# Weight tiles at fourteen addresses modulo 512 in a decoder layer on TensorE

## The chip, the cores and the metric

One NeuronCore of a Trainium2 chip runs the whole layer. The metric is the device time of one execution in microseconds (us). The engines are named as the profile names them: PE (TensorE matmuls), PEld (TensorE weight loads), DVE (VectorE), ACT (ScalarE), POOL (GpSimd) and SP, whose queue issues most DMAs.

## The reference

One layer of a hybrid decoder on x of 256 tokens by 2048 channels, all in float32:

```python
x = layer_norm(alpha * x + 0.5 * swiglu(x, w_gate1, w_up1, w_down1))        # d_ff = 5632
p = x @ w_in                                                                # 2048 x 6432
o_attn = diff_attn_group(p[..., :3072])      # 8 heads: softmax(s1) - lam * softmax(s2), then RMS norm
o_rwkv = rwkv7_group(p[..., 3072:])          # 16 heads of 64, delta-rule state over 256 tokens
x = layer_norm(alpha * x + concat(o_attn, o_rwkv) @ w_out)
x = layer_norm(alpha * x + 0.5 * swiglu(x, w_gate2, w_up2, w_down2))
```

Nearly all arithmetic is in the eight large products with weights; there are 350 MB of weights, read once.

## The kernel before, in words

**Split products.** Each float32 operand of a large product is split into a high and a low part of the type fp32r. A product is three matmuls: high x high (L105), low weight x high activation (L106), high weight x low activation (L107). The activations are the stationary operand (128 x 128, loaded by a weight load of PE), the weights the moving one (128 x 512). The two halves of 128 tokens are called tt 0 and tt 1.

**The weight stream.** `Stream.block` walks down a column of 512 weight columns in steps of two 128-row pieces. In each step SP loads a tile `raw` (512 KB), ACT rounds it to `wh` (L128), DVE subtracts to get `wl` (L129), and `mm` issues six matmuls for tt 0. The six for tt 1 come up to four steps later (`LAG`), so that PE reads two steps' buffers in turn. `raw` has 3 buffers, `wh` and `wl` 7 each (`NW`). A step thus takes 12 large matmuls, and there are 5856 with activations `xh` and `xl` as stationary operand (gate, up, `w_in`, `w_out`) and 2112 with the hidden activations `hh` (down).

**Stages.** FFN 1: gate and up blocks in turn, each pair ending in four transposes of `h` per token half (L221) and a split into `hh` tiles; then four down blocks; this twice, for 6 and for 5 groups of 512 hidden channels. Then the mixer: `w_in` blocks, with attention (`attn_heads`) and RWKV (`rwkv_group`) work put between the steps of the stream, and `w_out`. Then FFN 2 as FFN 1.

**Attention.** Two generators take two heads each and run in turn. A head's output goes from PSUM through `ot`: ACT squares into it (L803), DVE clips into it (L804), ACT squares it (L806), DVE writes the normed output (L817), PE transposes it (L821), DVE puts it over the query tile (L822). A scheduler orders each engine's instructions.

**Addresses.** Tiles lie at a byte address within each partition, and pools hand out addresses one tag after the other, so a tag's size sets the address of all that follow. One 128 x 128 slice of a stationary tile is 512 bytes, one piece of a weight tile 2048 bytes, so all slices of a tile have one address modulo 512:

| tiles | before | after |
|---|---|---|
| `xh`, `xl` (all 16) | 64 | 64 |
| `hh` J0, J1, J2 (both token halves), H0, H3 | 32 | 64 |
| `hh` H1, H4, H2, H5 | 64 | 64 |
| `raw` (3) | 64 | 64 |
| `wh` (7) | 64 | 64, 128, 192, ... 448 |
| `wl` (7) | 64 | 96, 160, 224, ... 480 |
| `ident` (moving tile of the transposes) | 128 | 128 |
| `h` (stationary tile of L221) | 480 | 416 |

Before, H3 has 4112 bytes in the mixer (`praw`), and that moves what follows from 32 to 64. In a block of a down stage, four of six (or four of five) groups of hidden channels are in tiles at 32. Of the 2112 matmuls of these stages 1536 have their stationary tile at 32 and 576 at 64.

Of the kernel before, what the change touches and what calls it, by code (L numbers as in the profile page):

```python
# [10 lines left out]
F32 = mybir.dt.float32  # L11
F32R = mybir.dt.float32r
# [4 lines left out]
P = 128  # L17
D = 2048
S = 256
DFF = 5632  # L20
NB = 512
# [10 lines left out]
NW = 7  # L32
# [5 lines left out]
def build(tc, A, out):  # L38
# [3 lines left out]
    hp = ctx.enter_context(tc.tile_pool(name="hp", bufs=1))  # L42
    xp = ctx.enter_context(tc.tile_pool(name="xp", bufs=1))
    wp = ctx.enter_context(tc.tile_pool(name="wp", bufs=1))
    sp = ctx.enter_context(tc.tile_pool(name="sp", bufs=2))
    dp = ctx.enter_context(tc.tile_pool(name="dp", bufs=1, space=bass.MemoryType.DRAM))
    pa = ctx.enter_context(tc.tile_pool(name="pa", bufs=3, space=bass.MemoryType.PSUM))

    HT = {"lw": "H0", "T1": "H1", "T2": "H2", "k": "H4"}
    uid = [0]  # L50

    def nm(s):
        uid[0] += 1
        return f"{s}_{uid[0]}"
# [31 lines left out]
    class Stream:  # L86
# [24 lines left out]
        def block(self, src, c0, w, ks, lhs, done, budget=0.0):  # L111
            blk = dict(ks=ks, w=w, lhs=lhs, done=done)
            for ki in range(0, len(ks), 2):
                for f in self.hooks.get(self.step, ()):
                    f()
                self.step += 1
                n = 2
                r0 = ks[ki][0]
                raw = wp.tile([P, n, NB], F32, tag="raw", name=nm("raw"), bufs=NRAW)
                wh = wp.tile([P, n, NB], F32R, tag="wh", name=nm("wh"), bufs=NW)  # L120
                wl = wp.tile([P, n, NB], F32R, tag="wl", name=nm("wl"), bufs=NW)
                g = 1 if self.step == 1 else n
                for k in range(0, n, g):
                    c = slice(k, k + g)
                    nc.sync.dma_start(out=raw[:, c, :w], in_=src[(r0 + k) * P:(r0 + k + g) * P, c0:c0 + w].rearrange("(k p) n -> p k n", p=P))
                for k in range(0, n, g):
                    c = slice(k, k + g)
                    SC.copy(out=wh[:, c, :w], in_=raw[:, c, :w])  # L128
                    V.tensor_tensor(out=wl[:, c, :w], in0=raw[:, c, :w], in1=wh[:, c, :w].bitcast(F32), op=ALU.subtract)  # L129
                st = (blk, ki, n, wh, wl)  # L130
                self.mm(st, 0)
                self.pend.append(st)
                if len(self.pend) > max(0, min(LAG, self.step // 4 - 1)):
                    self.mm(self.pend.pop(0), 1)
                self.run_bg(budget)
# [38 lines left out]
    def ln_tail(tt, y, st, gt, bt, last):  # L174
        mv = sp.tile([P, 2], F32, tag="mv", name=nm("mv"))
        V.bn_aggr(out=mv, in_=st)
        ve = sp.tile([P, 1], F32, tag="ve", name=nm("ve"))
        V.tensor_scalar(out=ve, in0=mv[:, 1:2], scalar1=LN_EPS, scalar2=None, op0=ALU.add)
        rs = sp.tile([P, 1], F32, tag="rs", name=nm("rs"))
        G.tensor_tensor(out=rs, in0=ve, in1=neghalf, op=ALU.pow)  # L180
        for q in range(4):
            c = slice(q * NB, (q + 1) * NB)
            yq = y[q]
            V.scalar_tensor_tensor(out=yq, in0=yq, scalar=mv[:, 0:1], in1=gt[:, c], op0=ALU.subtract, op1=ALU.mult)  # L184
            V.scalar_tensor_tensor(out=yq, in0=yq, scalar=rs, in1=bt[:, c], op0=ALU.mult, op1=ALU.add)  # L185
            if last:
                nc.sync.dma_start(out=out[tt * P:(tt + 1) * P, c], in_=yq)
            else:
                transpose_split(yq, tt, q, xT)
                nc.scalar.dma_start(out=xs[tt][:, c], in_=yq)  # L190

    def load_gb(pool, g, b, tg, tb, after=None):
        gt = (hp if tg == "J0" else pool).tile([P, D], F32, tag=tg, name=nm("lng"))
        bt = pool.tile([P, D], F32, tag=tb, name=nm("lnb"))
        if after is not None:
            G.tensor_copy(out=gt[:, 0:1], in_=after)
            G.tensor_copy(out=bt[:, 0:1], in_=after)
        nc.gpsimd.dma_start(out=gt, in_=g.to_broadcast([P, D]))
        nc.gpsimd.dma_start(out=bt, in_=b.to_broadcast([P, D]))
        return gt, bt  # L200

    def ffn(fp, wg, wu, wd, lg, lb, res, last, extra=None):
        y = [fp.tile([P, D], F32, tag=f"y{t}", name=nm("y")) for t in range(2)]
        st = [sp.tile([P, 4, 6], F32, tag=f"st{t}", name=nm("st"), bufs=1) for t in range(2)]
        gb = []
        j0 = 0
        for half, nj in enumerate((6, 5)):
            hT = {}
            sg = {}

            def gate_done(tt, acc):
                s = fp.tile([P, NB], F32, tag="sg", name=nm("sg"), bufs=2)
                SC.activation(out=s, in_=acc, func=AF.Silu)  # L213
                sg[tt] = s

            def up_done(tt, acc, j):
                h = fp.tile([P, NB], F32, tag="h", name=nm("h"), bufs=2)
                V.scalar_tensor_tensor(out=h, in0=sg[tt], scalar=0.5, in1=acc, op0=ALU.mult, op1=ALU.mult)  # L218
                tr = tr_bank[-1]()
                for i in range(4):  # L220
                    T.transpose(tr[:, i, :], h[:, i * P:(i + 1) * P], ident)  # L221
                if j < 3:
                    if tt == 0:
                        hT[j] = hp.tile([P, 4, 4, P], F32R, tag=f"J{j}", name=nm("hh"))
                    hi, lo = hT[j][:, 2 * tt], hT[j][:, 2 * tt + 1]
                else:
                    hl = hp.tile([P, 2, 4, P], F32R, tag=f"H{3 * tt + j - 3}", name=nm("hh"))
                    hi, lo = hl[:, 0], hl[:, 1]
                SC.copy(out=hi, in_=tr)  # L229
                V.tensor_tensor(out=lo, in0=tr, in1=hi.bitcast(F32), op=ALU.subtract)  # L230
                hT[(tt, j)] = (hi, lo)

            for j in range(nj):
                c0 = (j0 + j) * NB
                stream.block(wg, c0, NB, KX, x_lhs, gate_done)
                stream.block(wu, c0, NB, KX, x_lhs, lambda tt, acc, j=j: up_done(tt, acc, j))

            def h_lhs(tt, k, hT=hT):
                hi, lo = hT[(tt, k // 4)]
                return hi[:, k % 4, :], lo[:, k % 4, :]  # L240

            if half == 0 and extra is not None:
                extra(hT[(0, 0)][0][:, 0, 0:1].bitcast(F32))
            if half == 1:
                gb = load_gb(fp, lg, lb, "lng", "lnb", hT[(0, 0)][0][:, 0, 0:1].bitcast(F32))

            def down_done(tt, acc, n, half=half, hT=hT):
                c = slice(n * NB, (n + 1) * NB)
                if half == 0:
                    rc = fp.tile([P, NB], F32, tag="rc", name=nm("rc"), bufs=2)  # L250
                    G.tensor_copy(out=rc[:, 0:1], in_=hT[(0, 0)][0][:, 0, 0:1].bitcast(F32))
                    nc.scalar.dma_start(out=rc, in_=res[tt][:, c])
                    V.scalar_tensor_tensor(out=y[tt][:, c], in0=rc, scalar=ALPHA, in1=acc, op0=ALU.mult, op1=ALU.add)
                else:
                    V.tensor_tensor(out=y[tt][:, c], in0=y[tt][:, c], in1=acc, op=ALU.add)
                    V.bn_stats(out=st[tt][:, n, :], in_=y[tt][:, c])
                    if n == 3:
                        ln_tail(tt, [y[tt][:, i * NB:(i + 1) * NB] for i in range(4)], st[tt], gb[0], gb[1], last)

            for n in range(4):  # L260
                ks = [(j0 * 4 + k, k) for k in range(nj * 4)]
                stream.block(wd, n * NB, NB, ks, h_lhs, lambda tt, acc, n=n, f=down_done: f(tt, acc, n))
            j0 += nj
# [53 lines left out]
    def mix(mp, pq, C):  # L317
# [434 lines left out]
        def attn_heads(g, st, heads):  # L752
            q, k, vt = st["q"], st["k"], st["v"]
            W = 3 * P
            spans = [slice(0, P), slice(P, W)]
            for h in heads:
# [37 lines left out]
                T.matmul(po[:, 1, :], pT[:, 1, :], vt[0][:, hc], start=True, stop=False)  # L794
                T.matmul(po[:, 1, :], pT[:, 2, :], vt[1][:, hc], start=False, stop=True)

                ot = mp.tile([P, 2, P], F32, tag="ot", name=nm("ot"), bufs=2)
                ss = mp.tile([P, 2, 2], F32, tag="ss", name=nm("ss"), bufs=2)
                vr = mp.tile([P, 2, 2], F32, tag="vr", name=nm("vr"), bufs=2)
                fl = mp.tile([P, 2, 2], F32, tag="fl", name=nm("fl"), bufs=2)  # L800
# [149 lines left out]
```

## Time and profile before

| | |
|---|---|
| time, median of two runs | 2023.2 us (2022.15 and 2024.24) |
| time of the profiled execution | 2021.85 us |
| its span, from the first to the last instruction | 2020.1 us |
| mean granted TensorE clock | 0.989 of full speed |
| PE busy | 1976.9 us, 98% |
| PEld busy | 1614.6 us, 80% |
| DVE, ACT busy | 1149.0 us (57%), 887.6 us (44%) |

A row of a group reads: line, engine, operation, output <- inputs, tile shapes, count, then busy time in us, mean duration of one in ns, and the idle time of the engine just before them with what ended it. Durations of matmuls overlap, since a matmul's end is that of its last result; how fast they go is seen from the starts. A row of the timeline reads: start in us, length in us, engine, line, operation; equal neighbours are merged (x2). Buffer numbers are left out of names.

### The profile page before, as it was taken

Reading aid. Unit: us, or ns where it says so; the run is one execution under the profiler, and the core shown is the slowest. Engines: PE = TensorE matmul, PEld = TensorE weight load, DVE = VectorE, ACT = ScalarE, POOL = GpSimd, SP = SyncE. Lnnn points to the kernel's source line nnn. Section 1 sums busy time; section 2 is a strip of 40 time slices with the busy share of each in tenths; the row PEclk is TensorE's granted clock in tenths of the full one; section 3 lists DMA queues with packets and bytes.
Section 4 is the critical chain, followed back from the end, with each engine's and each line's share of the span. In section 5 each row is a group of like instructions: output and inputs, shape, how many; then the busy total and the mean of one; then the engine's idle time right before and its main releaser. Section 6 shows DMA issues by size and latency. Waiting matters only on the chain. (4 is left out here: it accounts for less than half of the span.)

```text
span 2020.1 us, 24928 instructions
## 1 busy us (share of the span) xinstructions
PE 1976.9 (98%) x9671; PEld 1614.6 (80%) x9671; DVE 1149.0 (57%) x1420; ACT 887.6 (44%) x1100; POOL 33.9 (2%) x68
## 2 busy tenths in 40 slices
PE   9999999999999999999999988999999999999997
PEld 7888888888888878888777777788888888888886
DVE  5555544445554566776677866755554444555455
ACT  5444433344444337645574444444443334444432
POOL 0200000000000000000000000000000000000000
PEclk9999999999999999999999979999999999999999
DMA  7766666667666556556435624666666666766553
GB/s 248 214 188 195 186 190 202 205 192 229 193 187 189 188 171 194 177 160 178 139 86 177 198 84 148 210 198 188 196 185 190 203 204 191 230 193 187 189 188 125
DMA packets 202008, 373.35 MB, mean 185 GB/s; under 512 B 22826, under 2 KB 24944, under 8 KB 201120
## 3 DMA queue, kind: packets, MB, share of 16 engines
q1 hardware_dynamic: 182928, 350.53, 58.0%
q10 hardware_dynamic: 17440, 14.29, 2.4%
q0 software_dynamic: 1520, 6.93, 1.0%
q8 instruction: 76, 1.25, 0.3%
q14 instruction: 44, 0.36, 0.1%
HBM read 364.10 MB, written 7.60 MB: 184 GB/s over the span
## 5 line engine op out<-in xcount | busy, mean ns | idle before, releaser
L129 DVE TENSOR_TENSOR wl<-raw,wh 128x1024 fp32r<-128x1024 f32 (+1 forms) x665 | 808.2, 1216 | 662.4 <-ACT wh L128 661.3
L128 ACT CAST wh<-raw 128x1024 fp32r<-128x1024 f32 (+1 forms) x665 | 695.2, 1046 | 851.9 <-PE acc L107 736.8
L107 PE MATMUL acc<-wh,xl 128*128 128x512 f32 (+1 forms) x1952 | 740.7, 391 | 1.6 <-DVE xl L79 1.6
L106 PE MATMUL acc<-wl,xh 128*128 128x512 f32 (+1 forms) x1952 | 736.7, 392 | 1.0 <-DVE wl L129 1.0
L105 PE MATMUL acc<-wh,xh 128*128 128x512 f32 (+1 forms) x1952 | 725.5, 392 | 9.0 <-ACT xh L78 7.6
L105 PEld LDWEIGHTS acc<-wh,xh 128*128 128x128 f32 x1952 | 367.9, 189 | 88.7 <-ACT xh L78 9.3
L106 PEld LDWEIGHTS acc<-wl,xh 128*128 128x128 f32 x1952 | 368.1, 189 | 77.5 <-issue 2.0
L107 PEld LDWEIGHTS acc<-wh,xl 128*128 128x128 f32 x1952 | 367.8, 188 | 76.3 <-DVE xl L79 2.0
L107 PE MATMUL acc<-wh,hh 128*128 128x512 f32 x704 | 258.0, 395 | 0.0
L106 PE MATMUL acc<-wl,hh 128*128 128x512 f32 x704 | 256.7, 394 | 0.0
L105 PE MATMUL acc<-wh,hh 128*128 128x512 f32 x704 | 256.0, 394 | 0.0
L106 PEld LDWEIGHTS acc<-wl,hh 128*128 128x128 f32 x704 | 132.0, 187 | 31.4
L107 PEld LDWEIGHTS acc<-wh,hh 128*128 128x128 f32 x704 | 132.0, 188 | 31.2
L105 PEld LDWEIGHTS acc<-wh,hh 128*128 128x128 f32 x704 | 132.0, 188 | 30.9
L230 DVE TENSOR_TENSOR hh<-tr,hh 128x512 fp32r<-128x512 f32 x44 | 30.4, 691 | 64.4 <-ACT hh L229 64.4
L229 ACT CAST hh<-tr 128x512 fp32r<-128x512 f32 x44 | 25.8, 586 | 91.7 <-PE tr L221 91.6
L218 DVE SCALAR_TENSOR_TENSOR h<-sg,acc 128x512 f32<-128x512 f32 x44 | 30.3, 688 | 35.6 <-PE acc L107 35.6
L213 ACT ACTIVATE sg<-acc 128x512 f32<-128x512 f32 x44 | 26.4, 600 | 43.8 <-PE acc L107 43.7
L577 DVE TENSOR_TENSOR itmp<-U,Y 64x31 f32<-64x31 f32 (+15 forms) x62 | 20.6, 332 | 11.5 <-DMA U<-dU 10.2
L221 PEld LDWEIGHTS tr<-ident,h 128*128 128x128 f32 x176 | 21.8, 139 | 5.7
L221 PE MATMUL tr<-ident,h 128*128 128x128 f32 x176 | 26.3, 272 | 0.0
L579 DVE TENSOR_TENSOR Y<-Y,itmp 64x31 f32<-64x31 f32 (+15 forms) x62 | 20.6, 332 | 1.4
(247 smaller groups left out, 750.2 us busy)
## 6 DMA issues: line engine op xcount, KB each, us to landing
raw<-in_ffn_w_up_dram SPq DMA_DIRECT2D x176, 512.0 KB, 3.9
raw<-in_ffn_w_down_dram SPq DMA_DIRECT2D x176, 512.0 KB, 4.1
raw<-in_ffn_w_gate_dram SPq DMA_DIRECT2D x175, 512.0 KB, 3.9
raw<-in_w_in_dram SPq DMA_DIRECT2D x96, 512.0 KB, 3.9
raw<-in_w_out_dram SPq DMA_DIRECT2D x32, 512.0 KB, 4.6
rc<-xs ACTq DMA_DIRECT2D x16, 256.0 KB, 4.0
lng<-in_ln_g_dram POOLq DMA_DIRECT2D x3, 1024.0 KB, 7.0
lnb<-in_ln_b_dram POOLq DMA_DIRECT2D x3, 1024.0 KB, 9.3
```

The costliest lines, as they stand in the source:

```text
L105: T.matmul(a, hi, wh[:, j, :w], start=(ki + j == 0), stop=False)
L106: T.matmul(a, hi, wl[:, j, :w], start=False, stop=False)
L107: T.matmul(a, lo, wh[:, j, :w], start=False, stop=(ki + j == last))
L128: SC.copy(out=wh[:, c, :w], in_=raw[:, c, :w])
L129: V.tensor_tensor(out=wl[:, c, :w], in0=raw[:, c, :w], in1=wh[:, c, :w].bitcast(F32), op=ALU.subtract)
L213: SC.activation(out=s, in_=acc, func=AF.Silu)
L218: V.scalar_tensor_tensor(out=h, in0=sg[tt], scalar=0.5, in1=acc, op0=ALU.mult, op1=ALU.mult)
L221: T.transpose(tr[:, i, :], h[:, i * P:(i + 1) * P], ident)
L229: SC.copy(out=hi, in_=tr)
L230: V.tensor_tensor(out=lo, in0=tr, in1=hi.bitcast(F32), op=ALU.subtract)
L577: V.tensor_tensor(out=tv, in0=U[:, 0:j, j:j + 1].to_broadcast([64, j, 32 - j]), in1=Y[:, j:j + 1, j:32].to_broadcast([64, j, 32 - j]), op= ...
L579: V.tensor_tensor(out=Y[:, 0:j, j:32], in0=Y[:, 0:j, j:32], in1=tv, op=ALU.add)
```

## The change

Each of the 7 `wh` and 7 `wl` buffers gets a tag of its own and 32 bytes more than it needs, in the order wh, wl, wh, wl, so that each starts 32 bytes (modulo 512) after the one before. The tag H3 is claimed first in its pool, with the 4128 bytes that it can need at most, and the `hh` tile in it starts 32 bytes in; so all `hh` tiles lie at 64. The 448 bytes and more that this takes are made up for by `ot`, which gets one buffer instead of two.

```diff
+    hp.tile([P, 4 * (S + 2)], F32, tag="H3", name="h3")
...
-                wh = wp.tile([P, n, NB], F32R, tag="wh", name=nm("wh"), bufs=NW)
-                wl = wp.tile([P, n, NB], F32R, tag="wl", name=nm("wl"), bufs=NW)
+                wh, wl = (wp.tile([P, n * NB + 8], F32R, tag=f"{t}{self.step % NW}", name=nm(t))[:, :n * NB].rearrange("p (k n) -> p k n", k=n)
+                          for t in ("wh", "wl"))
...
-                    hl = hp.tile([P, 2, 4, P], F32R, tag=f"H{3 * tt + j - 3}", name=nm("hh"))
-                    hi, lo = hl[:, 0], hl[:, 1]
+                    n = 3 * tt + j - 3
+                    o = 8 if n == 3 else 0
+                    hl = hp.tile([P, o + 8 * P], F32R, tag=f"H{n}", name=nm("hh"))
+                    hi, lo = [hl[:, o + c:o + c + NB].rearrange("p (a b) -> p a b", a=4) for c in (0, NB)]
...
-                ot = mp.tile([P, 2, P], F32, tag="ot", name=nm("ot"), bufs=2)
+                ot = mp.tile([P, 2, P], F32, tag="ot", name=nm("ot"))
```

The order of instructions is the same on every engine up to the middle of the mixer, and again from its end. Between, the single `ot` makes the scheduler put the second head of a pair behind the transposes of the first, and other work moves with it. (In the changed kernel lines stand two to four further down: L129 becomes L131, L804 L808, L821 L825.)

DVE, in the first pair of heads of the second attention group, before (`ot_9278` is the first head's, `ot_9292` the second's):

```order
L814 TENSOR_TENSOR ars_9282<-ars_9282,fl_9281 128x4
L129 TENSOR_TENSOR wl_9718<-raw_9716,wh_9717 128x1024
L804 TENSOR_SCALAR ot_9292<-at_9288 128x256
L815 TENSOR_TENSOR ars_9282<-ars_9282 128x2
L809 TENSOR_SCALAR vr_9294<-ss_9293 128x2
L812 TENSOR_SCALAR fl_9295<-ss_9293 128x2
L603 COPY PT_8548<-sm_8551 32x512
L129 TENSOR_TENSOR wl_9737<-raw_9735,wh_9736 128x1024
L817 TENSOR_SCALAR ot_9278<-at_9274,ars_9282 128x128 x2
```

The same place after (`ot_9279` and `ot_9293`):

```order
L818 TENSOR_TENSOR ars_9283<-ars_9283,fl_9282 128x4
L819 TENSOR_TENSOR ars_9283<-ars_9283 128x2
L821 TENSOR_SCALAR ot_9279<-at_9275,ars_9283 128x128 x2
L131 TENSOR_TENSOR wl_9719<-raw_9717,wh_9718 128x1024
L826 TENSOR_SCALAR qq<-at_9343,ng 128x256
L808 TENSOR_SCALAR ot_9293<-at_9289 128x256
L813 TENSOR_SCALAR vr_9295<-ss_9294 128x2
L816 TENSOR_SCALAR fl_9296<-ss_9294 128x2
L131 TENSOR_TENSOR wl_9738<-raw_9736,wh_9737 128x1024
```

The second head's clip (L804, now L808) stood ahead of the first head's last write to `ot`; now it stands behind that and behind the copy of the transposed first head into `qq`.

PE at the same place, before (L602, L613 and L623 are small products and transposes of the second RWKV group, L821 the transposes of `ot`):

```order
L602 MATMUL sm_8551<-YT_8547,Q 32x32 x32
L613 MATMUL sm_8588<-TT_8541,PT_8548 32x32
L623 MATMUL sm_8643<-ident,BKc 128x64 x8
L821 MATMUL at_9342<-ident,ot_9278 128x128 x2
L613 MATMUL sm_8588<-TT_8541,PT_8548 32x32 x31
L623 MATMUL sm_8653<-ident,BKc 128x64 x8
L623 MATMUL sm_8663<-ident,BKc 128x64 x8
L821 MATMUL at_9364<-ident,ot_9292 128x128 x2
```

And after:

```order
L825 MATMUL at_9343<-ident,ot_9279 128x128 x2
L606 MATMUL sm_8552<-YT_8548,Q 32x32 x32
L617 MATMUL sm_8589<-TT_8542,PT_8549 32x32
L627 MATMUL sm_8644<-ident,BKc 128x64 x8
L825 MATMUL at_9365<-ident,ot_9293 128x128 x2
L770 MATMUL at_9373<-k_8087,qq 128x128
L770 MATMUL at_9373<-k_8087,qq 128x256
L617 MATMUL sm_8589<-TT_8542,PT_8549 32x32 x31
```

The first head's transposes moved ahead of the RWKV group's products, and the second head's transposes ahead of 31 of them.

## The prediction

> **What bounds the kernel now.** The page comes first: the span, the engines' busy time, and the six groups of instructions that hold most of it.
>
> ```profile
> span 2020.1 us, 24928 instructions
> PE 1976.9 (98%) x9671; PEld 1614.6 (80%) x9671; DVE 1149.0 (57%) x1420; ACT 887.6 (44%) x1100; POOL 33.9 (2%) x68
> ...
> L107 PE MATMUL acc<-wh,xl 128*128 128x512 f32 (+1 forms) x1952 | 740.7, 391 | 1.6 <-DVE xl L79 1.6
> L106 PE MATMUL acc<-wl,xh 128*128 128x512 f32 (+1 forms) x1952 | 736.7, 392 | 1.0 <-DVE wl L129 1.0
> L105 PE MATMUL acc<-wh,xh 128*128 128x512 f32 (+1 forms) x1952 | 725.5, 392 | 9.0 <-ACT xh L78 7.6
> ...
> L107 PE MATMUL acc<-wh,hh 128*128 128x512 f32 x704 | 258.0, 395 | 0.0
> L106 PE MATMUL acc<-wl,hh 128*128 128x512 f32 x704 | 256.7, 394 | 0.0
> L105 PE MATMUL acc<-wh,hh 128*128 128x512 f32 x704 | 256.0, 394 | 0.0
> ```
>
> PE is idle for 2020.1 - 1976.9 = 43 us and almost never waits for a split weight. So the time is the number of large matmuls, 3 x 1952 + 3 x 704 = 5856 + 2112 = 7968, times the distance from one start to the next. Only that distance matters, and the mean durations above (391 to 395 ns) are not it, because matmuls overlap. The timeline of PE gives it. First a stretch in a gate or up block, from the first to the thirtieth matmul:
>
> ```profile
> 1408.31 0.39 PE L107 MATMUL acc<-wh,xl 128*128 128x512 f32 x1
> ...
> 1414.89 0.39 PE L107 MATMUL acc<-wh,xl 128*128 128x512 f32 x1
> ```
>
> 29 distances in 6.58 us: **227 ns**. Then a stretch in a down block, at a place where both token halves read J tiles, H0 or H3, thirty distances:
>
> ```profile
> 320.96 0.39 PE L105 MATMUL acc<-wh,hh 128*128 128x512 f32 x1
> ...
> 327.96 0.62 PE L107 MATMUL acc<-wh,hh 128*128 128x512 f32 x2
> ```
>
> 7.00 / 30 = **233 ns**. Same clock, same shapes, no wait in either. What differs is the address of the stationary tile modulo 512: in the gate block moving and stationary tile both lie at 64, an offset (moving minus stationary) of 0; in the down stretch they lie at 64 and 32, an offset of 32. The view of the instructions that use the weight tiles and the hidden tiles says the same in medians (minimum / median / maximum of a duration):
>
> ```profile
> L105 PEld LDWEIGHTS acc<-wh,xh x1952: 186/188/333, 6.8 to 1900.8; 128*128 128x128 f32 x196
> L105 PE MATMUL acc<-wh,xh x1952: 290/389/794, 6.8 to 1901.1; 128*128 128x512 f32 x193, 128*128 128x288 f32 x3
> ```
>
> ```profile
> L105 PEld LDWEIGHTS acc<-wh,hh x704: 187/188/192, 271.5 to 2007.2; 128*128 128x128 f32 x176
> L105 PE MATMUL acc<-wh,hh x704: 389/394/398, 271.8 to 2007.4; 128*128 128x512 f32 x176
> ...
> L106 PE MATMUL acc<-wl,hh x704: 387/394/397, 273.1 to 2007.7; 128*128 128x512 f32 x176
> ```
>
> A duration less 162 ns is the distance to the next start: 389 goes with 227, and 394 goes with 232, the down stages as a whole (1536 of their 2112 matmuls have the offset 32, the others 0). The weight load takes 188 ns in both, so it doesn't simply last longer; the stream of the running matmul is what is stretched while the next stationary tile is read.
>
> **Is 227 the good case or a bad one?** Two things bear on it. One is what happens at offset 0 after a disturbance. Behind eight small fp32 matmuls in the mixer the distances do not return to 227 at once:
>
> ```profile
> 875.63 1.89 PE L461 MATMUL sm<-lw,bones 128*128 128x256 f32 x8
> ...
> 877.59 0.39 PE L107 MATMUL acc<-wh,xl 128*128 128x512 f32 x1
> ...
> 879.67 0.39 PE L107 MATMUL acc<-wh,xl 128*128 128x512 f32 x1
> ```
>
> From 877.59 to 879.67 are nine distances, 2.08 / 9 = 231 ns, and only then does 227 come and stay. I read this as a state that settles: with one constant offset of 0 the stream and the load fall into a step that costs 227; out of step the same addresses cost 231. With the constant offset 32 they settle at 233. The other thing is the last large matmul ahead of a small one, whose stationary tile lies elsewhere. Windows around four of them, ahead of the transposes of h (offset 96), of the product with bones (128), of the transposes of s (480) and of the product with pT (288):
>
> ```profile
> L106 PE MATMUL acc<-wl,xh 128*128 128x512 f32 x1 | 0.4, 389 | 0.0
> ...
> L105 PE MATMUL acc<-wh,xh 128*128 128x512 f32 x1 | 0.4, 396 | 0.0
> ...
> L107 PE MATMUL acc<-wh,xl 128*128 128x512 f32 x1 | 0.4, 392 | 0.0
> ...
> L106 PE MATMUL acc<-wl,xh 128*128 128x512 f32 x1 | 0.4, 396 | 0.0
> ```
>
> Less 162 they are 227, 234, 230 and 234. The load that runs beside them is of another kind (fp32, partly a transpose), so they are weaker evidence, but none is under 227.
>
> **The change part by part.** The count of instructions and the bytes are the same; what goes is two sets of equal addresses.
>
> *Hidden tiles at 64 instead of 32.* If the weights stayed at 64, the 2112 matmuls of the down stages would come to 227: 2112 x 5 ns = 10.6 us less. That gain is not collected as such, because the moving tiles no longer lie at 64.
>
> *Fourteen moving addresses.* wh takes the offsets 0, 64, ... 384 and wl 32, 96, ... 416, and L105, L106, L107 use wh, wl, wh, of two different steps in turn (token half 0 of this step, half 1 of an earlier one). So the offset changes at nearly every matmul and no constant one can settle. I take the distances of the unsettled cases: 231 (behind the disturbance) and 233 (offset 32), so 232 ns for all. Gate, up, w_in and w_out blocks: 5856 x (232 - 227) = +29.3 us. Down blocks: 2112 x (232 - 232) = 0. Bounds, for the offsets that the trace doesn't show in these matmuls: the shortest duration among the hh rows, 387, gives 225, which is 5856 x -2 + 2112 x -7 = -26.5 us; the longest, 398, gives 236, which is 5856 x 9 + 2112 x 4 = +61 us. Farther down lies what eight fp32 matmuls with 256 columns need per start: (1.89 - 0.38) / 7 = 216 ns in the L461 row above, at offset 96 and without a visible stretch. If the large ones came down to it, the change would be 5856 x -11 + 2112 x -16 = -98 us. I take 232, which is nearest to the rows of these same matmuls.
>
> The Trainium skill speaks against the premise of the change: "TensorE: Matmul & The Clock Gate", section "Step-by-step: what each phase is for", says that moving operand and weight load have read ports of their own, and that "Loading the next tile's weights doesn't steal SBUF read bandwidth from the running matmul." By that rule addresses are of no account and the sum is 0. The two stretches above (227 and 233 ns at different addresses) do not agree with it.
>
> *ACT and DVE write and read the weight tiles at new addresses.* They show no such effect:
>
> ```profile
> L129 DVE TENSOR_TENSOR wl<-raw,wh 128x1024 fp32r<-128x1024 f32 x655 | 800.8, 1224 | 659.3 <-ACT wh L128 658.1
> ...
> L493 DVE TENSOR_TENSOR lw<-T,lw 128x1024 f32<-128x1024 f32 x2 | 2.4, 1224 | 0.0
> ```
>
> L129 has all three tiles at 64, L493 has T1 at 64 and lw at 32; both take 1224 ns. DVE is busy 57% of the span, so even 50 ns on each of 665 instructions (33 us in all) would lie beside PE. Cost 0. The DMAs into raw keep their addresses.
>
> *Attention output single.* The next head may write ot only after the transposes (L821) of the head before. In the pair of heads that bears on the end of the mixer:
>
> ```profile
> 1158.85 0.26 ACT L803 ACTIVATE ot<-at 128x128 f32<-128x128 f32 x1
> ...
> 1163.68 0.69 PE L821 MATMUL at<-ident,ot 128*128 128x128 f32 x2 [0.53 <-DVE ot L817]
> ...
> 1188.34 0.28 ACT L803 ACTIVATE ot<-at 128x128 f32<-128x128 f32 x1 [0.48 <-PE at L795]
> ...
> 1189.13 0.44 PE L821 MATMUL at<-ident,ot 128*128 128x128 f32 x2 [0.22 <-DVE ot L817]
> ...
> 1233.70 0.79 PE L105 MATMUL acc<-wh,xh 128*128 128x512 f32 x1 [5.90 <-ACT xh L78]
> ```
>
> The second head of the pair wrote at 1158.85 while the first was transposed at 1163.68 to 1164.4: it starts up to 5.5 us later. In the last pair it is 1.2 us (1188.34 against 1189.57). Queued behind the waiting ACT and DVE instructions are splits of weights, for which PE has several steps in store, and behind the second head's transposes on PE now 31 of the small products of the second RWKV group. Attention lateness is covered by the 5.90 us that PE sits idle before 1233.70 waiting for that RWKV group; lateness of the RWKV group itself is not covered. Between -3 (the first head's transposes now stand ahead of the RWKV products) and +5.5 us I take 0.
>
> **Sum.** +29.3 + 0 + 0. The profiled execution took 2021.85 us around its span of 2020.1; the median of the two runs, 2023.2, is 1.35 above, inside their spread. 2021.85 + 29.3 = 2051 us, 1.4% more.
>
> **The rivals.**
> - *Addresses don't matter, or only alignment of the stationary tile does.* Then the stretch at 233 ns belongs to the down stage and not to its addresses (2022 us), or the move to 64 collects its 10.6 us and the spread costs nothing (2011 us). For it: loads of 188 ns everywhere. Against it: 231 ns at offset 0 out of step. Chance 0.14. The rule of the Trainium skill ("TensorE: Matmul & The Clock Gate", quoted above) would give its first half.
> - *Spreading separates stream and load.* Equal addresses would be the collision and most of the fourteen offsets free; distances come towards 216, the time towards 2021.85 - 98 = 1924 us. It is faster by over 2% (40.5 us, 5.1 ns on each of 7968) once the mean is under 223.2 ns (now (5856 x 227 + 2112 x 232) / 7968 = 228.3). Against it: no large matmul row at another offset is under 227. Chance 0.10.
> - *Every offset but 0 costs as its worst moment.* The place is each matmul in turn, since each now meets a new offset; the longest distance shown in these rows, 236, gives +61 us, 2083 us. It counts as slower by over 2% from a mean of 233.4 ns, only 1.4 above my value. For it: 234 ahead of bones and pT. Chance 0.20.
>
> **How the numbers follow.** The forecast (226 to 233.4 ns without the first rival's reason) has 0.56; with the first rival's 0.14 that is 0.70 within 2%, which is about what a measurement of this kernel can tell from no change. Faster 0.10, slower 0.20. The range runs from 2005 us (a little under the alignment case) to 2083 us (236 everywhere); the collision-free case and what is left over it stay out.
>
> **What would show it.** Median durations of the large matmuls of 393 to 395 in both xh and hh groups, with a wide spread between single ones and no long stretch at one value, would bear out the step; 389 in both would be the alignment case; 378 to 385 in a good part the second rival; 396 and over the third. L129 should stay at 1224 ns. I would be wrong if distances at some offsets lie outside 225 to 236: the trace of before has no large matmul with an offset of 64 to 416 followed by another large one.

## The result: 1.4% slower, and the profile after

| | before | after |
|---|---|---|
| time, median of two runs | 2023.2 us | 2052.27 us (2051.72 and 2052.83) |
| ratio to before | | 1.0145, 95% interval 1.0125 to 1.0166 |
| span of the profiled execution | 2020.1 us | 2051.1 us |
| mean granted TensorE clock | 0.989 | 0.984 |

First the page of the changed kernel: the span, the engines' busy time and the groups that answer to the six shown of before (L107, L108 and L109 are L105, L106 and L107 of before), with the split on DVE.

```profile
span 2051.1 us, 24928 instructions
...
PE 2006.7 (98%) x9671; PEld 1622.5 (79%) x9671; DVE 1149.7 (56%) x1420; ACT 885.8 (43%) x1100; POOL 34.5 (2%) x68
...
L131 DVE TENSOR_TENSOR wl<-raw,wh 128x1024 fp32r<-128x1024 f32 (+1 forms) x665 | 808.0, 1216 | 682.0 <-ACT wh L130 681.4
...
L109 PE MATMUL acc<-wh,xl 128*128 128x512 f32 (+1 forms) x1952 | 746.1, 394 | 1.5 <-DVE xl L81 1.5
L108 PE MATMUL acc<-wl,xh 128*128 128x512 f32 (+1 forms) x1952 | 746.6, 397 | 0.6 <-DVE wl L131 0.4
L107 PE MATMUL acc<-wh,xh 128*128 128x512 f32 (+1 forms) x1952 | 732.8, 395 | 7.2 <-ACT xh L80 6.9
...
L108 PE MATMUL acc<-wl,hh 128*128 128x512 f32 x704 | 257.8, 395 | 0.0
L109 PE MATMUL acc<-wh,hh 128*128 128x512 f32 x704 | 257.4, 394 | 0.0
L107 PE MATMUL acc<-wh,hh 128*128 128x512 f32 x704 | 255.7, 393 | 0.0
```

PE is busy 30 us longer and still hardly waits for a weight tile. The three groups with xh or xl grew by 22.6 us together (that of wl with xh most, 736.7 to 746.6), the three with hh by 0.2. So most of the time went into the matmuls with xh and xl. The views of the instructions that use the weight tiles and the hidden tiles give the medians, 389 and 394 before:

```profile
L107 PE MATMUL acc<-wh,xh x1952: 292/393/797, 6.6 to 1932.2; 128*128 128x512 f32 x193, 128*128 128x288 f32 x3
...
L107 PE MATMUL acc<-wh,hh x704: 387/393/404, 276.8 to 2038.5; 128*128 128x512 f32 x176
```

And the timeline of PE in a gate or up block of FFN 2, the stage in which before showed 227 ns, from one matmul to the thirtieth after it:

```profile
1408.60 0.40 PE L108 MATMUL acc<-wl,xh 128*128 128x512 f32 x1
...
1415.56 0.40 PE L107 MATMUL acc<-wh,xh 128*128 128x512 f32 x1
```

6.96 / 30 = 232 ns. Taken over all undisturbed distances of the traces (from each start to the next where both matmuls are large, no other stands between and the distance is under 260 ns), the mean went from 227.3 to 231.7 ns with xh or xl as stationary operand, and from 232.0 to 231.9 ns with hh. Of those with xh or xl 87% were 226 or 227 ns before, up to 189 in a row; after it is 11%, and never more than two in a row. These figures come from the starts of the single matmuls in the two traces; no view prints them. The lower granted clock of the profiled execution (0.984) is not the cause: the change with two buffers of `ot`, below, has 0.989 and the same 231.7 ns.

### The profile page after: what moved, and what is told of

Read it like the earlier page. It is cut to its first block, busy times and chain, and to the rows that moved or that the text cites. A ratio compares the mean times of both kernels' runs of the same rounds, so it can differ in the third digit from the quotient of the medians.

```text
span 2051.1 us, 24928 instructions
## 1 busy us (share of the span) xinstructions
PE 2006.7 (98%) x9671; PEld 1622.5 (79%) x9671; DVE 1149.7 (56%) x1420; ACT 885.8 (43%) x1100; POOL 34.5 (2%) x68
## 5 line engine op out<-in xcount | busy, mean ns | idle before, releaser
L131 DVE TENSOR_TENSOR wl<-raw,wh 128x1024 fp32r<-128x1024 f32 (+1 forms) x665 | 808.0, 1216 | 682.0 <-ACT wh L130 681.4
L109 PE MATMUL acc<-wh,xl 128*128 128x512 f32 (+1 forms) x1952 | 746.1, 394 | 1.5 <-DVE xl L81 1.5
L108 PE MATMUL acc<-wl,xh 128*128 128x512 f32 (+1 forms) x1952 | 746.6, 397 | 0.6 <-DVE wl L131 0.4
L107 PE MATMUL acc<-wh,xh 128*128 128x512 f32 (+1 forms) x1952 | 732.8, 395 | 7.2 <-ACT xh L80 6.9
L107 PEld LDWEIGHTS acc<-wh,xh 128*128 128x128 f32 x1952 | 368.3, 189 | 94.7 <-ACT xh L80 8.5
L109 PEld LDWEIGHTS acc<-wh,xl 128*128 128x128 f32 x1952 | 368.2, 189 | 83.5 <-DVE xl L81 2.0
L108 PEld LDWEIGHTS acc<-wl,xh 128*128 128x128 f32 x1952 | 368.3, 189 | 83.1 <-DVE wl L131 1.6
L108 PE MATMUL acc<-wl,hh 128*128 128x512 f32 x704 | 257.8, 395 | 0.0
L109 PE MATMUL acc<-wh,hh 128*128 128x512 f32 x704 | 257.4, 394 | 0.0
L107 PE MATMUL acc<-wh,hh 128*128 128x512 f32 x704 | 255.7, 393 | 0.0
L107 PEld LDWEIGHTS acc<-wh,hh 128*128 128x128 f32 x704 | 132.2, 188 | 31.4
L109 PEld LDWEIGHTS acc<-wh,hh 128*128 128x128 f32 x704 | 132.2, 188 | 31.2
L108 PEld LDWEIGHTS acc<-wl,hh 128*128 128x128 f32 x704 | 132.2, 188 | 30.2
L233 ACT CAST hh<-tr 128x512 fp32r<-128x512 f32 x44 | 25.8, 586 | 94.0 <-PE tr L223 93.9
```

What stands on the lines that cost most here:

```text
L107: T.matmul(a, hi, wh[:, j, :w], start=(ki + j == 0), stop=False)
L108: T.matmul(a, hi, wl[:, j, :w], start=False, stop=False)
L109: T.matmul(a, lo, wh[:, j, :w], start=False, stop=(ki + j == last))
```

## The experiments

| kernel | median | ratio to before, 95% interval | undisturbed distance, mean |
|---|---|---|---|
| before | 2021.2 to 2025.0 in three series | | 228.6 ns |
| after | 2052.27 | 1.0145 (1.0125 to 1.0166) | 231.7 ns |
| all tiles at 64, `ot` with two buffers | 2010.15 | 0.9944 (0.9929 to 0.9958) | 226.9 ns in the FFNs |
| before with `ot` single | 2027.40 | 1.0025 (1.0015 to 1.0035) | 228.7 ns in FFN 1 |
| after with `ot` of two buffers | 2043.14 | 1.0107 (1.0090 to 1.0124) | 231.7 ns in the FFNs |
| `wl` at 96, the rest at 64, two `ot` | 2045.31 | 1.0103 (1.0086 to 1.0119) | 232.0 ns |
| all weight tiles at 192, two `ot` | 2049.48 | 1.0125 (1.0110 to 1.0140) | 232.7 ns |
| `wl` at 320, the rest at 64, two `ot` | 2009.30 | 0.9946 (0.9929 to 0.9962) | 226.9 ns in the FFNs |

The first experiments ask about the addresses (alone, then in the kernel), the last two about `ot`.

**One offset at a time.** A kernel of nothing but large matmuls, 48 for each offset, with stQ as stationary tile and moving tiles mvA to mvP at offsets 0, 32, ... 480 from it; stR lies 32 bytes behind stQ.

```diff
+    for m in mv:
+        for k in range(48):
+            T.matmul(acc, stat(k), half(m, k), start=False, stop=False)
```

> This kernel computes no layer: it only issues 1240 large fp32r matmuls on fixed tiles, with ACT and DVE idle, in parts: one constant offset (moving minus stationary address modulo 512) at a time, 0 to 480 in steps of 32, 48 matmuls each; offsets 0 and 32 with both tiles 32 bytes further on; offsets 0, 32, 0 in turn; the changed kernel's order of fourteen offsets; offset 0 again; offsets of 16, 8 and 4 bytes. Theory A (a constant offset settles into its own step, a changing one never does): each constant offset shows one value or a short repeating pattern, 227 at 0 and 233 at 32, the others in 225 to 236; offsets 0, 32, 0 in turn and the fourteen in turn give 231 to 232, more than the mean of the constant ones would explain. Theory B (each offset has a fixed price, no settling): the fourteen in turn give exactly the mean of the constant offsets, weighted 2 to 1 for the high parts. Theory C (the absolute alignment counts): with both tiles 32 bytes further on, offset 0 is dearer than 227.

The timeline of PE in that kernel; all 48 matmuls of a block are one row:

```profile
17.00 11.04 PE L54 MATMUL acc<-mvA,stQ 128*128 128x512 f32 x48
27.88 11.37 PE L54 MATMUL acc<-mvB,stQ 128*128 128x512 f32 x48
39.08 11.16 PE L54 MATMUL acc<-mvC,stQ 128*128 128x512 f32 x48
50.08 11.37 PE L54 MATMUL acc<-mvD,stQ 128*128 128x512 f32 x48
61.29 11.36 PE L54 MATMUL acc<-mvE,stQ 128*128 128x512 f32 x48
72.49 11.40 PE L54 MATMUL acc<-mvF,stQ 128*128 128x512 f32 x48
83.73 11.35 PE L54 MATMUL acc<-mvG,stQ 128*128 128x512 f32 x48
94.92 11.35 PE L54 MATMUL acc<-mvH,stQ 128*128 128x512 f32 x48
106.11 11.05 PE L54 MATMUL acc<-mvI,stQ 128*128 128x512 f32 x48
117.00 11.37 PE L54 MATMUL acc<-mvJ,stQ 128*128 128x512 f32 x48
...
195.23 11.09 PE L58 MATMUL acc<-mvB,stR 128*128 128x512 f32 x48
206.15 11.37 PE L58 MATMUL acc<-mvC,stR 128*128 128x512 f32 x48
...
228.50 0.40 PE L66 MATMUL acc<-mvA,stQ 128*128 128x512 f32 x1
...
272.91 11.05 PE L69 MATMUL acc<-mvA,stQ 128*128 128x512 f32 x48
```

The difference of two starts over 48 is the distance: offset 0 (27.88 - 17.00) 226.7 ns, offset 32 (39.08 - 27.88) 233.3, 64 229.2, 128 233.3, 160 (83.73 - 72.49) 234.2, and 256 (117.00 - 106.11) 226.9. From 256 on the row of values repeats. So the address counts modulo 256, not 512, and of the eight offsets in steps of 32 bytes only 0 and, in part, 64 are cheaper than 233. The two rows with stR settle what "offset" is: with stR the moving tile at mvB is the one at offset 0, and it costs 227.5 over the block (the first ten matmuls run unsettled at 224 to 236, the rest at 226.7), while mvC costs 233.3. It is the relation of the two addresses that counts, not either one alone. Offsets 0, 32 and 0 in turn gave 232.2, not the 228.9 that a mean of the two settled values would be: there theory A holds and theory B fails. With the changed kernel's order of fourteen offsets (192 matmuls from L66 to L69) it is the other way round: (272.91 - 228.50) / 192 = 231.3, and the mean of the fourteen settled values, the high parts counted twice, is 231.3 as well. So the change of offset costs extra in short turns of 0 and 32, but adds nothing for the fourteen. Theory C falls with the 226.7 at stR.

**What the relation is not.** A second kernel of this kind varies the load.

```diff
+        T.matmul(acc[0:64], stat(k)[:, 0:64], half(mv[0], k), start=False, stop=False, skip_group_check=True)
...
+        T.matmul(acc, (stat, stat2)[k % 2](k // 2), half(mv[(k + 1) % 2], k // 2), start=False, stop=False)
```

> No layer is computed: large fp32r matmuls alone, as in the first such kernel, 48 for each part. (1) Offset 0 with stationary tiles of 128, 64 and 32 columns, (2) the same at offset 32: if it is the reading of the next stationary tile that stretches the running stream, the distance falls from 226.7 (and 233.3) towards 216 as the load gets shorter, about half of the excess with 64 columns; if the excess belongs to the stream alone, it stays. (3) Offsets 0 and 256 in turn: 226.7, if the period is 256 bytes; 0 and 64 in turn: 230 or more (never settled), though the mean of the two settled values is 227.8. (4) Stationary tiles at two addresses 32 bytes apart in turn, the moving tile at that of the next one's, then (5) at that of its own: if it is the running stream against the next load, (4) settles at 226.7 and (5) doesn't. (6) Every second column of a wider stationary tile: more lines read per load, more than 226.7. (7) 256 moving columns: not predicted, over 108. (8) The kernel's order with addresses in steps of 256 instead of 32: 226.7 as one address.

Its timeline, first with 128, 64 and 32 stationary columns at offset 0 (mvA) and at offset 32 (mvB), then with 256 moving columns at offset 0:

```profile
16.95 11.04 PE L55 MATMUL acc<-mvA,stQ 128*128 128x512 f32 x48
27.82 11.20 PE L57 MATMUL acc<-mvA,stQ 128*64 128x512 f32 x48
38.86 11.29 PE L59 MATMUL acc<-mvA,stQ 128*32 128x512 f32 x48
49.98 11.35 PE L62 MATMUL acc<-mvB,stQ 128*128 128x512 f32 x48
61.17 11.24 PE L64 MATMUL acc<-mvB,stQ 128*64 128x512 f32 x48
72.25 11.05 PE L66 MATMUL acc<-mvB,stQ 128*32 128x512 f32 x48
...
138.50 5.91 PE L83 MATMUL acc<-mvA,stQ 128*128 128x256 f32 x48
```

At offset 0 the distances are 226.5, 230.0 and 231.7 ns: a shorter load makes them longer. At offset 32 they are 233.1, 230.8 and, over the matmuls of the last block, 226.8. So the stretch isn't simply the length of the load beside the stream; the number of columns shifts which offset is cheap. Two stationary tiles in turn, with the moving tile at the next one's address, gave 230.0, and with it at its own tile's address 231.8. If only the running stream and the load beside it counted, one of the two would have stood at 226.7. That simple picture falls, and the runs put no other in its place. Offsets 0 and 256 in turn settled at 226.7, and the changed kernel's order in steps of 256 bytes gave 226.8. Offsets 0 and 64 in turn gave 231, and every second column of a wider stationary tile 233.3; these four came as expected.

**All tiles at 64.** The change without its 32 extra bytes and with both buffers of `ot`, which leaves only the move of the `hh` tiles to 64.

```diff
-                wh, wl = (wp.tile([P, n * NB + 8], F32R, tag=f"{t}{self.step % NW}", name=nm(t))[:, :n * NB].rearrange("p (k n) -> p k n", k=n)
+                wh, wl = (wp.tile([P, n * NB], F32R, tag=f"{t}{self.step % NW}", name=nm(t))[:, :n * NB].rearrange("p (k n) -> p k n", k=n)
...
-                ot = mp.tile([P, 2, P], F32, tag="ot", name=nm("ot"))
+                ot = mp.tile([P, 2, P], F32, tag="ot", name=nm("ot"), bufs=2)
```

> The changed kernel without the 32 bytes of padding in the weight buffers and with two buffers for the attention output: all moving and all stationary tiles at 64. Theory A and B: every large matmul at offset 0, medians 389 (227 ns) in the down stages too, 2112 x 5 ns = 10.6 us less than before, about 2012 us. If the down stages are slower for another reason than the address (the stage, the hidden tiles' layout), 2023 us as before.

2010.15 us, 0.9944 of before, and faster than both kernels. The view of the instructions that use its hidden tiles, with 394 in before:

```profile
L107 PE MATMUL acc<-wh,hh x704: 387/389/397, 272.2 to 1995.3; 128*128 128x512 f32 x176
```

**Two addresses, one address elsewhere, and 256 bytes apart.** Three placements with one stationary address and two buffers of `ot`. In the first a pad of 32 bytes puts `wl` at 96; in the second a pad of 128 bytes ahead of `raw` puts all weight tiles at 192; in the third the pad ahead of `wl` has 256 bytes and puts it at 320. The pad lines of the three edits, in this order:

```diff
+                    wp.tile([P, 8], F32, tag="pad", name="pad")
...
+    wp.tile([P, 32], F32, tag="pad", name="pad")
...
+                    wp.tile([P, 64], F32, tag="pad", name="pad")
```

> As the kernel with all tiles at 64 (2010 us), but all wl at 96: offsets 0, 32, 0 in turn. Theory A (changing offsets don't settle, 232 ns as in the part of the micro kernel with 0, 32, 0 in turn): 7968 x 5.3 = +42 us, 2052 us, as much as fourteen addresses cost. Theory B (a fixed price for each offset, 226.7 for two of three and 233.3 for the third, mean 228.9): +18 us, 2028 us.

> As the kernel with all tiles at 64 (2010 us), but raw, wh and wl all at 192: one constant offset of 128, which settles at 233.3 ns in the micro kernel. Both theories: 7968 x 6.6 = +53 us, 2063 us, more than fourteen addresses cost. If it were only the change from address to address that costs, 2010 us.

> All wh tiles at 64, all wl tiles at 320, all stationary tiles at 64, ot with two buffers: the offset alternates irregularly between 0 and 256, as it alternated between 0 and 32 with wl at 96 (2045.31 us). If what counts is the offset modulo 256, the distance is that of offset 0 throughout: medians of 389 ns in both the xh and the hh groups, a mean of 226.9 ns, and the time of the kernel with all tiles at 64, 2010 us (2008 to 2013). If it is the offset modulo 512, or any change of offset, the matmuls stay unsettled: mean 231 to 232 ns, medians of 393 to 395, 2040 to 2046 us.

2045.31, 2049.48 and 2009.30 us. Below stand the group of hidden matmuls with the low weight part, from the groups by line of the first (its mean was 394 in before), and the view of the instructions that use the hidden tiles of the third:

```profile
L108 PE MATMUL acc<-wl,hh 128*128 128x512 f32 x704 | 258.7, 397 | 0.0
```

```profile
L107 PE MATMUL acc<-wh,hh x704: 387/389/397, 272.6 to 1994.5; 128*128 128x512 f32 x176
```

Two addresses 32 bytes apart cost as much as fourteen (1.0103 and 1.0107 of before). One address for all weight tiles at a constant offset of 128 costs more still than those two (2049.48 us, in the same series), though nothing changes from one matmul to the next. And two addresses 256 bytes apart, in the same irregular turns as 64 and 96, cost nothing (2009.30 against 2010.15). So the number of addresses isn't what costs, and a change of offset costs nothing as long as each is 0 modulo 256. What costs is offsets that aren't 0 modulo 256, and where they stand among matmuls at 0, those lose their cheap distance too: with a third of the matmuls at 32 the mean is 232.0, where the settled values alone would give 228.9.

The two-address kernel came under its 2052 and the one at 192 under its 2063 by 7 and 14 us. Over the whole program the mean distance rose from 227.1 ns (all tiles at 64) by 4.9 and 5.6, not by 5.3 and 6.6; of these 39 and 45 us the spans show 36 and 39.

**The attention output.** Before with a single `ot`, and the change with two:

```diff
-                ot = mp.tile([P, 2, P], F32, tag="ot", name=nm("ot"), bufs=2)
+                ot = mp.tile([P, 2, P], F32, tag="ot", name=nm("ot"))
```

> The kernel before with one buffer for the attention output and nothing else. The prediction's term: 0 (between -3 and +5.5 us), 2023 us. Rival: the mixer's excess (the changed kernel's trace has a wait of 6.4 us of PE at 1173 us, behind the second transposes of the attention output, which before has not) comes from this edit: +4 to +6 us, 2028 us.

> The changed kernel with two buffers for the attention output: the fourteen addresses alone. Prediction: the whole +29 us is of the addresses, 2052 us as the changed kernel. Rival: the single attention output carries 4 to 6 us of it, 2047 us.

The single `ot` alone costs 0.25% (0.15 to 0.35), some 5 us (3 to 7). The change with two came out at 2043.14 us, below the 2052 of the prediction and below the rival's 2047 as well. So in the changed kernel the single `ot` is 2052.27 - 2043.14 = 9 us, and the spans say 9.9; the intervals of the two ratios leave room for 0 to 15, so this isn't shown to differ from 5. A place where it could come in shows in the timeline of ACT behind the last pair of heads of the first attention group. Before:

```profile
1021.03 1.06 ACT L693 ACTIVATE Q<-BKc 128x1024 f32<-128x1024 f32 x1
...
1026.01 1.28 ACT L700 ACT_TABLE_LOAD   x1 [1.16 <-PE sm L699]
...
1032.26 0.84 ACT L485 ACTIVATE lw<-sm,vB 128x256 f32<-128x256 f32 x2
...
1048.27 1.06 ACT L517 ACTIVATE Q<-Q 128x1024 f32<-128x1024 f32 x1
```

Before with a single `ot`:

```profile
1024.10 1.06 ACT L693 ACTIVATE Q<-BKc 128x1024 f32<-128x1024 f32 x1 [2.46 <-DVE BKc L690]
1026.35 0.28 ACT L803 ACTIVATE ot<-at 128x128 f32<-128x128 f32 x1 [1.20 <-PE at L821]
...
1028.19 1.28 ACT L700 ACT_TABLE_LOAD   x1
...
1034.77 0.84 ACT L485 ACTIVATE lw<-sm,vB 128x256 f32<-128x256 f32 x2
...
1052.83 1.06 ACT L517 ACTIVATE Q<-Q 128x1024 f32<-128x1024 f32 x1
```

The second head's L803 waits for the first head's transposes at L821. Behind it in ACT's order stand, with their table loads, the activations for the output norm of the first RWKV group (L700) and for the decay of the second (L485); they start 2.2 and 2.5 us later. But that is not shown to be the wait's doing: L693, which stands ahead of L803, is already 3.1 us late, and by the starts in the two traces the large matmuls run 1.9 us behind from 800 us on, where the edit has not moved anything yet. The pair of the change with two `ot` and the changed kernel has no such lag there (0.1 us). First the change with two:

```profile
1038.94 1.28 ACT L704 ACT_TABLE_LOAD   x1 [1.16 <-PE sm L703]
...
1045.19 0.84 ACT L489 ACTIVATE lw<-sm,vB 128x256 f32<-128x256 f32 x2
...
1061.19 1.06 ACT L521 ACTIVATE Q<-Q 128x1024 f32<-128x1024 f32 x1
```

Then the changed kernel:

```profile
1039.17 1.28 ACT L704 ACT_TABLE_LOAD   x1
...
1045.75 0.84 ACT L489 ACTIVATE lw<-sm,vB 128x256 f32<-128x256 f32 x2
...
1063.81 1.06 ACT L521 ACTIVATE Q<-Q 128x1024 f32<-128x1024 f32 x1
```

Here the same two (L704 and L489) are only 0.2 and 0.6 us later; L521 (L517 of before), in the chain of the second RWKV group, is 2.6 us later. The delay gathers farther on. PE meets it at the product that needs that group's solved matrix. Its rows before, and before with a single `ot`:

```profile
1157.80 1.54 PE L602 MATMUL sm<-YT,Q 32*32 32x32 f32 x64 [1.71 <-DMA YT<-dYT]
```

```profile
1167.89 2.15 PE L602 MATMUL sm<-YT,Q 32*32 32x32 f32 x64 [6.67 <-DMA YT<-dYT]
```

And in the change with two `ot`, and the changed kernel:

```profile
1169.73 0.24 PE L606 MATMUL sm<-YT,Q 32*32 32x32 f32 x2 [0.52 <-DMA YT<-dYT]
```

```profile
1179.42 0.31 PE L606 MATMUL sm<-YT,Q 32*32 32x32 f32 x2 [6.15 <-DMA YT<-dYT]
```

The product is 10.1 and 9.7 us later, and PE's idle time ahead of it goes from 1.71 to 6.67 us and from 0.52 to 6.15. So with a single `ot` PE waits some 5 us longer for the second RWKV group. What makes that group late wasn't taken apart by a run of its own: the wait at L803 is one candidate, the new order of the other work in the mixer another.

## Why the prediction was right, and where its terms were not

The forecast was 2051 us, the measurement 2052.27. The cause named, the addresses, is the one the runs show, but that the sum came so close is luck: two errors cancel.

- **The bound.** Matmul count times distance, with everything else hidden, holds for most of the program: placements alone moved the time between 2009.30 and 2049.48 us. It does not hold in the second half of the mixer, as the next term shows.
- **Address term, +29.3 us.** It measured 21.6 us (the change with two `ot`, 1.07% of 2021.85, interval 18 to 25). The step that was mis-sized is the pair of distances. The forecast took 227 and 232 for xh; the means are 227.3, since PE runs unsettled for a while after an interruption (mostly six to ten matmuls), and 231.7. That is 5856 x 4.4 = 25.8 us, and 2112 x -0.1 = -0.2 for hh. Of these 25.6 us the span shows 2041.2 - 2020.1 = 21.1. The rest is lost in the mixer: by their starts in the traces, the large matmuls of the change with two `ot` fall behind those of before by 12.6 us up to 971 us, are 12.2 us behind at 1320, and go on to 21.1 at the end. In the stretch between, PE's idle time went from 22.5 to 19.6 us: there PE waits for other work, and the slower matmuls cost nothing.
- **Why it costs.** "No constant one can settle" was the reason given for 232. The value held, the reason mostly not: the fourteen cost 231.3 alone, just the mean of their fourteen constant offsets, a constant offset of 128, at which nothing changes, gave 232.7 in the kernel, and changing offsets of 0 and 256 gave 226.9. Leaving offset 0 modulo 256 is what costs; that the offset changes as well counts where 0 and 32 take turns. Nor is it shown that the stream is stretched "while the next stationary tile is read": at offset 0 a shorter load made the distance longer (226.5, 230.0, 231.7). Why the relation of the two addresses costs time stays open.
- **Hidden tiles, -10.6 us if the weights stayed.** All tiles at 64 took 0.56% less (0.42 to 0.71), 8.5 to 14.4 us. This step is borne out.
- **ACT and DVE at new addresses, 0.** L131 takes 1223 ns for a 128x1024 tile against 1224 of L129, and PE's waits for wl add up to 0.4 us. Borne out.
- **Attention output, 0 of a range from -3 to +5.5 us.** It measured +3 to +7 alone. The step that failed is the price of nothing for a late RWKV group. The sentence "lateness of the RWKV group itself is not covered" named the risk, and PE's wait for that group grew by some 5 us (1.71 to 6.67, and 0.52 to 6.15). "Queued behind the waiting ACT and DVE instructions are splits of weights" left out that in another pair, the last of the first attention group, activations and table loads of the RWKV groups stand there too; that these carried the delay isn't shown.
- **The sum.** 2021.85 + 21.6 + 5 to 9 gives 2048 to 2052.

The rivals: that addresses don't matter, or only that of the stationary tile, fell with the one-offset kernel, where the stationary tile stood still. That spreading separates stream and load fell there too: none of sixteen offsets is under 226.7, the value of equal addresses. That every offset costs 236 fell there as well, with 234.2 as the dearest of the sixteen; the median of 393 is under the 396 set for it.

The rule quoted from the Trainium skill ("TensorE: Matmul & The Clock Gate", section "Step-by-step: what each phase is for"), that loading the next weights doesn't steal read bandwidth from the running matmul, would have given equal rows for mvA and mvB. The rows differ by 6.6 ns, so for these matmuls with a load each the measurement decides against using it as "addresses are of no account". What the two sides share the runs do not show.

## What to carry to other kernels

Where fp32r matmuls of 128x512 with a 128x128 load each are the bound, put moving and stationary tiles at one address modulo 256 bytes; here that took 0.56% off, in a kernel in which 1536 of 7968 matmuls had lain 32 bytes off. For narrower stationary tiles another offset can be the cheap one (32 for 32 columns). A buffer taken from a side chain to pay for it isn't free because that chain has slack: the new wait changes the order of other work too, and a third chain can be the one that ends last. And a total that comes out right doesn't bear out its terms; only runs with one part of the change at a time did.

## What the runs showed that was not expected

- The period is 256 bytes: the distances at offsets 0, 32, ... 224 (226.7, 233.3, 228.9, 233.3, 233.3, 234.2, 233.3, 233.3 ns once settled) repeat from 256 on.
- Offset 64 has a value of its own, 228.9, and offsets smaller than 32 bytes aren't cheap: 16 and 8 bytes gave 231.7, 4 bytes 236.7.
- Fewer stationary columns made the matmuls at offset 0 slower (226.5, 230.0, 231.7 ns for 128, 64, 32), and those at offset 32 faster.
- 256 moving columns at offset 0 took (144.24 - 138.50) / 48 = 119.6 ns, more than half of 226.7 by 6.3 ns; so a part of each distance, about 12.5 ns if the rest goes with the columns, may belong to the matmul and not to its columns. But PEld was idle for only 0.1 us in that part, so the loads may be what set the 119.6; no run separates the two.
